# FFN input products of a two-layer trunk as seven block products, with a separate output stage

## The chip, the cores and the metric

One program runs on one core of one Trainium2 chip. The time is device microseconds (us) of one execution; less is better. TensorE (PE in the profile, its weight loads PEld) multiplies, VectorE (DVE), ScalarE (ACT) and GpSimd (POOL) do the elementwise work, SyncE (SP) issues most DMAs. All operands are float32 in DRAM.

## What is computed

The reference is a trunk of two layers over 1024 tokens of width 1024. Each layer has a token mixer (a gated DeltaNet, then a dilated window attention), and after it a SwiGLU feed-forward network (FFN) with 2816 hidden units. What the change touches is the FFN:

```python
h = (rms_norm(x, norm_ffn[layer]) * (1.0 + sc2) + sh2).astype(x.dtype)
x = x + g2 * swiglu(h, w_ffn_in[layer], w_ffn_out[layer])

def swiglu(h, w_in, w_out):
    gate, up = jnp.split(h @ w_in, 2, axis=-1)
    return (jax.nn.silu(gate) * up) @ w_out
```

## The kernel before

Activations are kept transposed: features on the 128 partitions, 512 tokens (one of two halves) along a row, so x is 2 x 8 tiles of 128x512. Every product is made in split float32: an operand is a pair of an upper part `hi` (ACT copies it, rounded to float32r) and a lower part `lo` (the rest, one subtraction in `lo_of`, which goes to DVE and to POOL in turn, since `lo_pool` is 2 in the FFN). `split3` sums upper x upper, upper x lower and lower x upper: three matmuls for each 128 of the contraction.

The FFN (`ffn`) goes through 22 tiles of 128 hidden units in groups of 2 or 3 (`FG`). For each tile `gate_up` multiplies gate and up weights with the first token half and then with the second, 24 matmuls of 128x128 by 128x512 into each PSUM bank, applies SiLU and the product with up, and splits the result for the next product. Once a group is through, its output products follow at once: 16 banks of three matmuls per tile, each added to x by one DVE instruction (L1141). In layer 0, `mods1` also works through the 96 pieces of the next layer's conditioning (one 256 KB load and one DVE instruction each, L221 and L223), three after each `gate_up`.

Which instruction stands where on each engine is decided by a scheduler at build time, from the order in the code; each engine then runs its own list strictly in order and waits on semaphores. While `PE.pinned` is set, PE's instructions keep the order of the code. Tiles come from pools with a fixed number of buffers, so a load can wait for the last reader of a buffer. `hlp` holds 32 tiles of 128x512, that is 16 pairs.

Of the kernel before, what the change touches and what calls it, by code (L numbers as in the profile page):

```python
# [17 lines left out]
P = 128  # L18
# [53 lines left out]
def trunk(tc, A, out, stop=None):  # L72
# [3 lines left out]
    class PE:  # L76
# [217 lines left out]
    def row_bcast(p, r, n=4):  # L294
# [3 lines left out]
        rb = p.tile([P, HALF], F32, name="rb", tag="rb", bufs=2)  # L298
        ACT.activation(rb, b, AF.Copy)
        return rb  # L300
# [155 lines left out]
    class OutProj:  # L456
# [51 lines left out]
        def late(self, tp, xp):  # L508
            w0 = [wunit(rows_cols(self.w_out, n * P, P), KT) for n in (3, 3 + 1)]
            self.ws = dict(zip((3, 3 + 1), w0))  # L510
            xT = [[xp.tile([P, HALF], F32, name="xt", tag="xt", bufs=16) for _ in range(KT)] for _ in range(2)]
# [3 lines left out]
            rb0 = row_bcast(tp, self.r0)  # L515
            stat = Stat(tp)
# [7 lines left out]
            return xT, [rb0, stat.r()]  # L524
# [573 lines left out]
    FG = [2, 2] + [3] * 6  # L1098

    def ffn(tp, xT, l, hT, tail, between=None):  # L1100

        w_i, w_o = A["w_ffn_in"][l], A["w_ffn_out"][l]
        t0 = 0
        for gi, gn in enumerate(FG):
            acts = [[None] * gn for _ in range(2)]
            wg = [None] * gn
            wo = []

            def gate_up(i, hf):
                t = t0 + i  # L1110
                if wg[i] is None:
                    wg[i] = (wunit(rows_cols(w_i, t * P, P), KT),
                             wunit(rows_cols(w_i, HID + t * P, P), KT))
                og, ou = pd(), pd()
                for o, w in ((og, wg[i][0]), (ou, wg[i][1])):
                    split3(o, [((w[0][:, k], w[1][:, k]), hT[hf][k]) for k in range(KT)])
                s = tp.tile([P, HALF], F32, name="sg", tag="ft")
                ACT.activation(s, og, AF.Silu)  # L1118
                V.tensor_tensor(s, s, ou, ALU.mult)  # L1119
                hi = tp.tile([P, HALF], F32R, name="ahi", tag="act", bufs=14)  # L1120
                lo = tp.tile([P, HALF], F32R, name="alo", tag="act", bufs=14)
                ACT.activation(hi, s, AF.Copy)  # L1122
                lo_of(lo, s, hi)
                acts[hf][i] = (hi, lo)
            order = [(i, hf) for i in range(gn) for hf in range(2)]
            if gi == 0:
                order = [(0, 0), (1, 0), (0, 1), (1, 1)]
            for i, hf in order:
                gate_up(i, hf)
                if between is not None:  # L1130
                    between()
            for i in range(gn):
                t = t0 + i
# [10 lines left out]
            t0 += gn  # L1144
    def toks(g, t):
# [22 lines left out]
    lo_pool, accs, araw = 2, 3, 3  # L1168
    with ExitStack() as fa:
        banks(pd="ab", pt="de", p0="a", p1="b", p2="c")  # L1170
        fw = fa.enter_context(pool("fw", 3))
        wpools(fw, 3, 1, 3)
        xp = fa.enter_context(pool("xp"))
        tp = fa.enter_context(pool("ft", 5))
        xT, rb = op.late(tp, xp)
        hT = [make_h(tp, 0, 1, xT[hf], rb[hf]) for hf in range(2)]
# [7 lines left out]

        ends = []
# [341 lines left out]
```

## Time and profile before

| | |
|---|---|
| three runs | 3048.33, 3054.59, 3058.15 us (median 3054.59) |
| the profiled execution | 3051.78 us, of which 3050.0 us lie between its first and last instruction (the span) |
| mean granted TensorE clock in it | 0.967 of full |

The rows further down come from this one execution. A row of busy times gives an engine's share of a stretch; a row of a timeline gives the start of a run of like instructions, how long it took, and in brackets how long the engine had been idle before it and whose work ended that.

### The profile page before, as it was taken

To read this page: it belongs to the slowest core of one execution; us is meant where nothing else is said; L and a number is where in the kernel's file an instruction comes from. 1 tells how busy PE (TensorE), PEld (TensorE's weight loads), DVE (VectorE), ACT (ScalarE), POOL (GpSimd) and SP (SyncE) were. 2 spreads that over 40 slices of the span, in tenths; PEclk is the share of its full clock that TensorE was granted. 3 is DMA by queue.
4 is the path that set the end of the run, shared out by engine and by line. 5 is a ranking of instruction groups with operands and counts; after the bars stand their busy time and mean duration, and the time that the engine had idled before them with its cause. 6 is when DMAs were issued, how large, how long until landed. Compare 5 with 4: busy or idle time off the path is not lost.

```text
span 3050.0 us, 39919 instructions
## 1 busy us (share of the span) xinstructions
PE 2900.4 (95%) x15831; PEld 2459.7 (81%) x15831; DVE 1375.7 (45%) x2799; ACT 877.3 (29%) x1779; POOL 667.1 (22%) x626
## 2 busy tenths in 40 slices
PE   6889888898989999999999999999979999999999
PEld 5777777776878888888879899999968888888887
DVE  7775676656686423222245342333276322332222
ACT  5432333333421211111134453443334121111111
POOL 2141323331211111111124122222212111111110
PEclk7989999999999999999999999999979999999999
DMA  7333332236765311111122301111222111111111
GB/s 252 96 94 115 105 87 66 55 100 187 234 205 156 104 42 49 40 58 49 49 80 81 99 29 41 52 50 44 77 91 73 45 56 42 50 41 55 49 35 59
DMA packets 271447, 250.91 MB, mean 82 GB/s; under 512 B 32035, under 2 KB 214563, under 8 KB 271260
## 3 DMA queue, kind: packets, MB, share of 16 engines
q1 hardware_dynamic: 265612, 234.77, 25.7%
q0 software_dynamic: 5648, 13.60, 1.5%
q8 instruction: 124, 2.03, 0.3%
q14 instruction: 63, 0.52, 0.1%
HBM read 218.70 MB, written 34.30 MB: 83 GB/s over the span
## 4 chain that ended last, share of the span: by engine, by line
PE 67%; DMA 3%; DVE 3%; issue 1%; ACT 0%; SPq 0%; POOL 0%; DVEq 0%; ACTq 0%; POOLq 0%
PE pd L82 59%; PE pt L82 3%; PE ob L82 2%; PE pp L82 1%; PE p L82 1%; DMA araw<-in_w_ada 1%; PE tq L82 1%; DMA b_d<-v_d 1%; DVE acc L223 1%; DVE w L157 0%; DMA gl<-og_d 0%; DVE ht L307 0%; DMA xt<-xs_d 0%; DVE hl L315 0%; DMA wraw<-in_dsw_w_in 0%
## 5 line engine op out<-in xcount | busy, mean ns | idle before, releaser
L82 PE MATMUL pd<-hl,w 128*128 128x512 f32 x6360 | 1550.1, 400 | 18.2 <-ACT w L183 9.1
L82 PEld LDWEIGHTS pd<-hl,w 128*128 128x128 f32 x6360 | 1196.4, 192 | 265.6 <-ACT w L183 9.7
L183 ACT ACTIVATE w<-wraw 128x512 fp32r<-128x512 f32 (+1 forms) x363 | 260.5, 730 | 877.2 <-PE pd L82 341.2
L157 POOL TENSOR_TENSOR w<-wraw,w 128x512 fp32r<-128x512 f32 (+1 forms) x135 | 225.9, 1675 | 1190.0 <-ACT w L183 1149.5
L82 PE MATMUL pd<-ahi,w 128*128 128x512 f32 x1408 | 451.5, 398 | 2.6 <-DVE xt L1141 2.6
L157 DVE TENSOR_TENSOR w<-wraw,w 128x512 fp32r<-128x512 f32 (+1 forms) x228 | 208.9, 919 | 386.9 <-ACT w L183 371.7
L82 PE MATMUL pd<-w,hl 128*128 128x256 f32 x2880 | 377.0, 286 | 0.0
L82 PEld LDWEIGHTS pd<-w,hl 128*128 128x128 f32 x2880 | 355.4, 192 | 7.2 <-issue 6.0
L82 PEld LDWEIGHTS pd<-ahi,w 128*128 128x128 f32 x1408 | 265.1, 188 | 66.2 <-DVE xt L1141 3.1
L82 PE MATMUL pd<-alo,w 128*128 128x512 f32 x704 | 279.4, 397 | 0.0
L1119 DVE TENSOR_TENSOR sg<-sg,pd 128x512 f32<-128x512 f32 x88 | 60.3, 685 | 383.6 <-PE pd L82 379.1
L82 PEld LDWEIGHTS pd<-alo,w 128*128 128x128 f32 x704 | 132.7, 188 | 31.3
L1141 DVE SCALAR_TENSOR_TENSOR qkv<-pd,modT,qkv 128x512 f32<-128x512 f32 x128 | 95.5, 750 | 128.6 <-PE pd L82 128.5
L223 DVE SCALAR_TENSOR_TENSOR acc<-araw,vecT,acc 128x512 f32<-128x512 f32 x140 | 113.3, 809 | 59.0 <-DMA araw<-in_w_ada 57.5
L1141 DVE SCALAR_TENSOR_TENSOR xt<-pd,modT,xt 128x512 f32<-128x512 f32 x128 | 95.0, 748 | 97.6 <-PE pd L82 97.4
L1118 ACT ACTIVATE sg<-pd 128x512 f32<-128x512 f32 x88 | 52.4, 596 | 242.4 <-PE pd L82 242.4
L1122 ACT ACTIVATE ahi<-sg 128x512 fp32r<-128x512 f32 x88 | 55.2, 627 | 221.8 <-DVE sg L1119 220.5
L682 DVE SCALAR_TENSOR_TENSOR yv<-raw,vecT,yv 128x512 f32<-128x512 f32 x144 | 112.6, 782 | 10.7 <-ACT yv L680 9.7
L135 POOL TENSOR_TENSOR ssa<-ssa,pw 128x8 f32<-128x8 f32 x48 | 80.7, 1682 | 165.8 <-DVE ssa L1304 154.5
L157 POOL TENSOR_TENSOR alo<-sg,ahi 128x512 fp32r<-128x512 f32 x46 | 67.0, 1456 | 212.3 <-ACT ahi L1122 212.2
L1346 DVE CUSTOM_DVE_ANT_0 p<-pt,bias 128x256 f32<-128x256 f32 (+1 forms) x192 | 61.6, 370 | 99.3 <-PE pt L82 63.4
L1352 ACT ACTIVATE p<-p,nm 128x256 f32<-128x256 f32 (+1 forms) x192 | 87.4, 457 | 36.8 <-DVE nm L1349 29.5
(285 smaller groups left out, 2746.5 us busy)
## 6 DMA issues: line engine op xcount, KB each, us to landing
araw<-in_w_ada SPq DMA_DIRECT2D x160, 256.0 KB, 2.9
wraw<-in_w_ffn_in SPq DMA_DIRECT2D x54, 512.0 KB, 3.9
wraw<-in_dsw_w_in SPq DMA_DIRECT2D x72, 256.0 KB, 2.9
wraw<-in_w_ffn_in SPq DMA_DIRECT2D x68, 256.0 KB, 2.9
wraw<-in_gdn_w_in SPq DMA_DIRECT2D x66, 256.0 KB, 2.9
wraw<-in_w_ffn_out SPq DMA_DIRECT2D x26, 512.0 KB, 3.8
wraw<-in_w_ffn_out SPq DMA_DIRECT2D x36, 256.0 KB, 2.6
araw<-in_w_ada SPq DMA_DIRECT2D x16, 512.0 KB, 8.4
```

What stands on the lines that cost most here:

```text
L82: i = f(*a, **k)
L135: G.tensor_tensor(o, i, pw[:, half, :n], ALU.pow)
L157: e.tensor_tensor(o, x, hi.bitcast(F32), ALU.subtract)
L183: ACT.activation(hi, raw, AF.Copy)
L223: V.scalar_tensor_tensor(acc, raw, condT[:, k:k + 1], acc, op0=ALU.mult, op1=ALU.add)
L682: V.scalar_tensor_tensor(yv, raw[:, i:i + HALF], convT[:, i, ct:ct + 1], yv, op0=ALU.mult, op1=ALU.add)
L1118: ACT.activation(s, og, AF.Silu)
L1119: V.tensor_tensor(s, s, ou, ALU.mult)
L1122: ACT.activation(hi, s, AF.Copy)
L1141: V.scalar_tensor_tensor(xt, o, modT[:, l, 5, n:n + 1], xt, op0=ALU.mult, op1=ALU.add)
L1346: V.tensor_tensor_reduce(p_[i][:, hp, c0:], lg[i][:, hp * 256 + c0:hp * 256 + 256], bias[:, h, c0:], 1.0, -3.0e38, ALU.add, ALU.max, orow[ ...
L1352: ACT.activation(p_[i][:, hp, c0:], p_[i][:, hp, c0:], AF.Exp, bias=nm[:, h:h + 1], accum_out=orow[:, h, DH + 1:DH + 2])
```

## The change

The gate and up weights of one hidden tile are taken as two rows of blocks (gate, up) by two columns (features 0 to 511, 512 to 1023), h as two rows of blocks (the same feature halves) by two columns (the token halves). The 2x2 block product is formed from seven block products (Winograd's form of Strassen's method) in place of eight, each of four 128-deep steps of three matmuls: 12 matmuls. Numbers 1 and 2 use blocks of weights and of the first token half as they are; 3, 4, 5, 6 and 7 need sums and differences of blocks of the weights, of h, or of both.

- `half0` makes h of the first token half (one DVE product with the row factors, one ACT instruction for the rest, in place in x) and its 8 pairs. `begin` then does products 1 and 2 of tiles 0 and 1.
- After that come the statistics of the second token half, its h, the block differences of h, and the 20 pairs of products 7, 6, 5, 3 and 4 (`half1`).
- `rest` does all other products in a written order, PE pinned. `weights` forms the weights' sums and splits them, `taken` empties the banks: partial results are copied out between products that go on adding to the same bank.
- The activations go to DRAM (`a_d`). Since x was overwritten by h, x goes to DRAM as well (`xs_d`) and comes back. All 22 tiles are through before the output stage (`ffn_out`) starts: it loads the activations, splits them, and multiplies in groups of 3 or 4 tiles.
- In layer 0 the conditioning pieces go one to a product from the ninth product of `rest` on, with two load buffers in place of three.

```diff
...
+        def then(cls, o, wh, wl, hh, hl, first, last):
+            cls.matmul(o, wh, hh, start=first, stop=False, skip_group_check=True)
+            cls.matmul(o, wh, hl, start=False, stop=False, skip_group_check=True)
+            cls.matmul(o, wl, hh, start=False, stop=last, skip_group_check=True)
...
-        def late(self, tp, xp):
-            w0 = [wunit(rows_cols(self.w_out, n * P, P), KT) for n in (3, 3 + 1)]
-            self.ws = dict(zip((3, 3 + 1), w0))
-            xT = [[xp.tile([P, HALF], F32, name="xt", tag="xt", bufs=16) for _ in range(KT)] for _ in range(2)]
+        def late(self, tp, w_from):
+            wcyc[0] = cycle([w_from])
+            self.ws = dict((n, wunit(rows_cols(self.w_out, n * P, P), KT)) for n in (3, 4))
+            xT = [[tp.tile([P, HALF], F32, name="xt", tag="ft") for _ in range(KT)] for _ in range(2)]
             for hf, ns in ((1, range(3)), (0, range(KT)), (1, range(3, KT))):
                 for n in ns:
                     SP.dma_start(xT[hf][n], xs_d[hf, n])
-            rb0 = row_bcast(tp, self.r0)
-            stat = Stat(tp)
+            rb0 = row_bcast(tp, self.r0, bufs=1)
+            stat = Stat(None, *(tp.tile([P, HALF], F32, name="sq", tag="ft") for _ in range(2)))
             for n in range(KT):
                 xt = xT[1][n]
                 if n < 3:
...
                 else:
                     self.one(n, 1, xt)
                 stat.add(xt)
-            return xT, [rb0, stat.r()]
+                G.dma_start(xs_d[1, n], xt)
+            return xT, rb0, stat
+    class FfnIn:
+        def __init__(self, l, ft, hx, fw, raws):
+            self.l, self.ft, self.hx, self.fw, self.raws = l, ft, hx, fw, raws
+            self.B = {x: [] for x in range(1, 8)}
+            self.st = [dict() for _ in range(NHT)]
+        def pair(self, x, far):
+            if far:
+                t = self.hx.tile([P, 2, HALF], F32R, name="hx", tag="hx")
+                hi, lo = t[:, 0], t[:, 1]
+            else:
+                hi, lo = hl_tile()
+            ACT.activation(hi, x, AF.Copy)
+            lo_of(lo, x, hi)
+            return hi, lo
+        def h(self, k, x, rb):
+            V.tensor_tensor(x, x, rb, ALU.mult)
+            ACT.activation(x, x, AF.Identity, bias=modT[:, self.l, 3, k:k + 1], scale=AT_[:, self.l, 1, k:k + 1])
+        def half0(self, xs, rb):
+            self.x0 = xs
+            for k in range(KT):
+                self.h(k, xs[k], rb)
+                self.B[1 if k < 4 else 2].append(self.pair(xs[k], False))
+        def half1(self, xs, rb):
+            x0, x1, ft = self.x0, xs, self.ft
+            for k in range(4):
+                self.h(k, x1[k], rb)
+                self.h(k + 4, x1[k + 4], rb)
+                V.tensor_tensor(x0[k], x1[k], x0[k], ALU.subtract)
+                V.tensor_tensor(x1[k], x1[k + 4], x1[k], ALU.subtract)
+                self.B[7].append(self.pair(x1[k], True))
+                ft.give(x1[k])
+            for k in range(4):
+                t = ft.take()
+                V.tensor_tensor(t, x1[k + 4], x0[k], ALU.subtract)
+                self.B[6].append(self.pair(t, True))
+                G.tensor_tensor(x0[k + 4], x0[k + 4], t, ALU.subtract)
+                ft.give(t)
+            for x, far, ts in ((5, True, x0[:4]), (3, False, x1[4:]), (4, False, x0[4:])):
+                for t in ts:
+                    self.B[x].append(self.pair(t, far))
...
+        def op(self, x):
+            w = self.fw.tile([P, 2, HALF], F32R, name="wo", tag="wo")
+            ACT.activation(w[:, 0], x, AF.Copy)
+            lo_of(w[:, 1], x, w[:, 0])
+            return w[:, 0], w[:, 1]
+        def weights(self, i, x):
+            s, ft = self.st[i], self.ft
+            if x in (1, 2):
+                if x == 1:
+                    s["rg"], s["ru"] = self.raw(i * P), self.raw(HID + i * P)
+                    w = s["w"] = wps.tile([P, 2, 1024], F32R, name="w", tag="w")
+                    ACT.activation(w[:, 0], s["rg"], AF.Copy)
+                    lo_of(w[:, 1], s["rg"], w[:, 0])
+                c = slice((x - 1) * HALF, x * HALF)
+                return s["w"][:, 0, c], s["w"][:, 1, c]
+            a11, a12, a21, a22 = (t[:, j * HALF:(j + 1) * HALF] for t in (s["rg"], s["ru"]) for j in range(2))
+            if x == 7:
+                t = ft.take()
+                V.tensor_tensor(t, a11, a21, ALU.subtract)
+                r = self.op(t)
+                ft.give(t)
+            elif x == 6:
+                s["s1"], s["s2"] = ft.take(), ft.take()
+                G.tensor_tensor(s["s1"], a21, a22, ALU.add)
+                V.tensor_tensor(s["s2"], s["s1"], a11, ALU.subtract)
+                r = self.op(s["s2"])
+            elif x == 5:
+                r = self.op(s["s1"])
+                ft.give(s["s1"])
+            elif x == 3:
+                V.tensor_tensor(s["s2"], a12, s["s2"], ALU.subtract)
+                r = self.op(s["s2"])
+                ft.give(s["s2"])
+            else:
+                r = self.op(a22)
+        def product(self, i, x):
+            s = self.st[i]
+            wh, wl = self.weights(i, x)
+            key = {2: "y", 4: "v", 7: "v"}.get(x, "u")
+            first, last = x in (1, 2, 7), x in (2, 3, 4)
+            if first:
+                s[key] = bank[key]()
+            for k, (hh, hl) in enumerate(self.B[x]):
+                c = slice(k * P, (k + 1) * P)
+                PE.then(s[key], wh[:, c], wl[:, c], hh, hl, first and k == 0, last and k == 3)
+            self.taken(i, x, s[key])
...
+        def begin(self):
+            for i in range(2):
+                for x in (1, 2):
+                    self.product(i, x)
+        def rest(self, between=None):
+            seq = [(i, x) for x in (7, 6, 5) for i in range(2)] + [(0, 3), (0, 4), (2, 1), (1, 3), (1, 4)]
+            for i in range(2, NHT):
+                seq += [(i, 7), (i, 6), (i, 2), (i, 5)] + [(i + 1, 1)] * (i + 1 < NHT) + [(i, 3), (i, 4)]
+            for n, (i, x) in enumerate(seq):
+                self.product(i, x)
+                if between is not None and n >= 8:
+                    between()
+    FG = [3, 4, 4, 4, 4, 3]
+    def ffn_out(l, xT, act_raw, tail):
...
+            wo, acts = [], [[], []]
+            for t in range(t0, t0 + gn):
+                for hf in range(2):
+                    r = act_raw()
+                    SP.dma_start(r, a_d[t, hf])
+                    hi, lo = hl_tile()
+                    ACT.activation(hi, r, AF.Copy)
+                    lo_of(lo, r, hi)
+                    acts[hf].append((hi, lo))
...
+            tp = f1.enter_context(pool("ft", 18))
+            xT, rb0, stat1 = op.late(tp, (wps, 1, (fw, "wraw", 4)))
+            ff = FfnIn(0, Slotted(tp), hx, fw, lambda: fw.tile([P, 1024], F32, name="wraw", tag="wraw", bufs=4))
+            ff.half0(xT[0], rb0)
+            banks(u="aad", v="b", y="c", pt="e")
+            PE.pinned = True
+            ff.begin()
+            PE.pinned = False
+            rb = row_bcast(tp, stat1.factors(tp.tile([P, 2, 4], F32, name="rst", tag="rst", bufs=1)), bufs=1)
+            ff.half1(xT[1], rb)
+            ends, calls = [], [0]
+            mods = [f for j in (1, 0, 2, 4, 3, 5)
+                    for f in mod_pieces(tp, 1, j, lambda f: ends.append((calls[0] + 3, f)), "ft")]
+            def mods1():
+                calls[0] += 1
+                while ends and ends[0][0] <= calls[0]:
+                    ends.pop(0)[1]()
+                if mods:
+                    mods.pop(0)()
+            PE.pinned = True
+            ff.rest(mods1)
+            while mods or ends:
+                mods1()
+            PE.pinned = False
+        fw = fa.enter_context(pool("fw", 6))
+        wpools(fw, 6, 1, 3)
+        tp = fa.enter_context(pool("ft", 8))
+        xT = [[xp.tile([P, HALF], F32, name="xt", tag="xt", bufs=16) for _ in range(KT)] for _ in range(2)]
+        for hf in range(2):
+            for n in range(KT):
+                SP.dma_start(xT[hf][n], xs_d[hf, n])
...
+    ff, ring = end["ff"], end["ft"]
+    with ExitStack() as f1:
+        banks(u="aad", v="b", y="c", pt="e")
+        ff.hx = f1.enter_context(pool("hx", 12))
+        ff.fw = fw = f1.enter_context(pool("fw", 6))
+        own = [lambda: fw.tile([P, 1024], F32, name="wraw", tag="wraw", bufs=2)] * 2
+        rcyc = cycle(own + [lambda r=r: r for r in end["raws"]])
+        ff.raws = lambda: next(rcyc)()
+        PE.pinned = True
+        ff.begin()
+        PE.pinned = False
+        rb = row_bcast(end["slots"], end["stat"].factors(ssx[:, :, 0:4]))
+        ff.half1(xT[1], rb)
+        PE.pinned = True
+        ff.rest()
...
```

Three places in the built order follow. `u`, `v` and `y` are PSUM banks of the block products, `hx` pairs of block differences of h, `wo` the split of a weight sum, `ft` scratch tiles, `ar` activations read back.

On PE at the start of layer 0's FFN, first before (the 171 begin with the last five output products of the mixer, 120 matmuls), then after the change:

```order
L82 MATMUL pd<-hl,w 128x512 x171
L82 MATMUL pt<-sq,sqa 128x1 x4
L82 MATMUL pd<-hl,w 128x512 x34
L82 MATMUL pt<-sq,rst 128x128 x4
L82 MATMUL pd<-hl,w 128x512 x11
```

```order
L82 MATMUL pd<-hl,w 128x512 x120
L82 MATMUL u<-hl,w 128x512 x12
L82 MATMUL y<-hl,w 128x512 x12
L82 MATMUL u<-hl,w 128x512 x12
L82 MATMUL y<-hl,w 128x512 x12
L82 MATMUL pt<-sq 128x1 x4
L82 MATMUL pt<-sq,rst 128x128 x4
L82 MATMUL v<-hx,wo 128x512 x24
```

The sums of the second half's statistics (`128x1`) stood after one product of the FFN with the first half, with more behind them; now they stand after everything that the first half alone allows, and products with `hx` are next.

On DVE and on POOL at the same place, after the change: from the row factors of the second half on (DVE), and from behind the square root of its statistics (POOL). L1156 and L1170 to L1178 are `half1` and `h`, L164 is `lo_of`, L1209 and L1214 the weights' sums:

```order
L1156 TENSOR_TENSOR xt<-xt,rb 128x512 x8
L1170 TENSOR_TENSOR xt<-xt 128x512 x3
L1171 TENSOR_TENSOR xt<-xt 128x512 x2
L164 TENSOR_TENSOR hl<-xt,hl 128x512
L1171 TENSOR_TENSOR xt<-xt 128x512
L1170 TENSOR_TENSOR xt<-xt 128x512
L164 TENSOR_TENSOR hx<-xt,hx 128x512
L164 TENSOR_TENSOR hl<-xt,hl 128x512
L1171 TENSOR_TENSOR xt<-xt 128x512
L1176 TENSOR_TENSOR ft<-xt 128x512 x4
L164 TENSOR_TENSOR hx<-xt,hx 128x512
L1209 TENSOR_TENSOR ft<-wraw 128x512 x2
```

```order
L164 TENSOR_TENSOR hl<-xt,hl 128x512 x2
L164 TENSOR_TENSOR hx<-xt,hx 128x512 x2
L1178 TENSOR_TENSOR xt<-xt,ft 128x512 x2
L164 TENSOR_TENSOR hx<-ft,hx 128x512
L1178 TENSOR_TENSOR xt<-xt,ft 128x512 x2
L1214 TENSOR_TENSOR ft<-wraw 128x512
L164 TENSOR_TENSOR hx<-ft,hx 128x512
L164 TENSOR_TENSOR hl<-xt,hl 128x512
L164 TENSOR_TENSOR hx<-xt,hx 128x512 x2
L164 TENSOR_TENSOR wo<-ft,wo 128x512
```

POOL's last row is the lower part of the weights of product 7 of tile 0, which PE's first run of `v<-hx,wo` reads in its third matmul. On DVE, six more lower parts follow the rows shown, the sixth that of product 7 of tile 1: 32 instructions in all. In layer 1, whose rows are not shown, DVE has 32 as well, and POOL 16 in front of the same row where it has 14 here.

On SP at the end of layer 0's input stage, before (weights of both products alternate), and after:

```order
L181 DMA wraw<-in_w_ffn_in 128x4x128 x3
L181 DMA wraw<-in_w_ffn_in 128x8x128 x3
L181 DMA wraw<-in_w_ffn_in 128x4x128 x4
L179 DMA wraw<-in_w_ffn_out 128x1024 x2
L181 DMA wraw<-in_w_ffn_in 128x8x128
```

```order
L1255 DMA a_d<-ft 128x512
L186 DMA wraw<-in_w_ffn_out 128x1024 x3
L1261 DMA a_d<-ft 128x512
L186 DMA wraw<-in_w_ffn_out 128x1024
L1368 DMA xt<-xs_d 128x512 x16
L1289 DMA ar<-a_d 128x512 x8
```

The store of the last tile's activations, and sixteen loads of x, now stand ahead of the first activation that is read back. The fourth `128x1024` load reuses the first one's buffer.

## Rows read from the trace of the kernel before

**Rows 1.** The page, busy time, share of the span and number of instructions.

```profile
PE 2900.4 (95%) x15831; PEld 2459.7 (81%) x15831; DVE 1375.7 (45%) x2799; ACT 877.3 (29%) x1779; POOL 667.1 (22%) x626
```

**Rows 2.** Stretches: length, busy PE, PEld, DVE, ACT, POOL; granted clock, DMA share, GB/s.

```profile
843.00:900.00 57.00, 53.04 (x248) 43.47 (x246) 44.63 (x68) 16.02 (x23) 9.91 (x6) 0.97 0.63 192
900.00:1400.00 500.00, 497.22 (x2191) 408.07 (x2192) 187.29 (x240) 84.91 (x124) 79.74 (x47) 1.00 0.26 78
...
2420.00:3000.00 580.00, 580.00 (x2533) 475.62 (x2532) 157.06 (x188) 99.98 (x146) 90.14 (x54) 1.00 0.15 45
```

**Rows 3.** Timeline of PE in layer 1: FFN input, and output product of the mixer.

```profile
2377.30 43.70 PE L82 MATMUL pd<-hl,w 128*128 128x512 f32 x192
2420.83 0.40 PE L82 MATMUL pd<-ahi,w 128*128 128x512 f32 x1
...
2270.20 5.74 PE L82 MATMUL pd<-hl,w 128*128 128x512 f32 x24
2275.78 0.38 PE L82 MATMUL pp<-sq,m 128*128 128x128 f32 x2
...
2292.79 29.27 PE L82 MATMUL pd<-hl,w 128*128 128x512 f32 x127
2321.90 0.94 PE L82 MATMUL pt<-sq,qkv 128*128 128x1 f32 x8
```

**Rows 4.** Timeline of layer 1's statistics of the second half, all engines.

```profile
2324.56 1.01 POOL L135 TENSOR_TENSOR rst<-rst,pw 128x4 f32<-128x4 f32 x1 [1.43 <-DVE rst L340]
...
2328.52 1.05 PE L82 MATMUL pt<-sq,rst 128*128 128x128 f32 x8
...
2329.61 0.60 ACT L299 ACTIVATE qkv<-pt 128x512 f32<-128x512 f32 x1 [0.47 <-PE pt L82]
```

**Rows 5.** The activations' lower parts: nanoseconds least/median/most, first and last start.

```profile
L157 POOL TENSOR_TENSOR alo<-sg,ahi x46: 1278/1295/2007, 864.1 to 3005.5; 128x512 fp32r<-128x512 f32 x46
L157 DVE TENSOR_TENSOR alo<-sg,ahi x42: 679/693/2574, 902.7 to 2994.6; 128x512 fp32r<-128x512 f32 x42
```

**Rows 6.** Timeline of DVE and POOL in layer 0.

```profile
826.54 0.75 DVE L307 SCALAR_TENSOR_TENSOR ht<-xt,modA,rb 128x512 f32<-128x512 f32 x1
...
826.88 3.87 POOL L157 TENSOR_TENSOR w<-wraw,w 128x1024 fp32r<-128x1024 f32 x1 [7.85 <-ACT w L183]
827.81 0.69 DVE L157 TENSOR_TENSOR w<-wraw,w 128x512 fp32r<-128x512 f32 x1
...
828.41 2.90 DVE L315 SCALAR_TENSOR_TENSOR hl<-ht,modT,hl 128x512 fp32r<-128x512 f32 x1
```

**Rows 7.** Groups by line and shape: busy us, mean ns, idle before.

```profile
L157 POOL TENSOR_TENSOR w<-wraw,w 128x1024 fp32r<-128x1024 f32 x41 | 102.4, 2500 | 423.4 <-ACT w L183 423.4
L183 ACT ACTIVATE w<-wraw 128x1024 fp32r<-128x1024 f32 x87 | 90.4, 1054 | 257.7 <-PE pd L82 138.4 <-issue 114.1 <-DMA wraw<-in_gdn_w_out 3.9
L1122 ACT ACTIVATE ahi<-sg 128x512 fp32r<-128x512 f32 x88 | 55.2, 627 | 221.8 <-DVE sg L1119 220.5 <-issue 0.8
L223 DVE SCALAR_TENSOR_TENSOR acc<-araw,vecT,acc 128x512 f32<-128x512 f32 x140 | 113.3, 809 | 59.0 <-DMA araw<-in_w_ada 57.5
```

**Rows 8.** SP's timeline where x is loaded; then DMA issues: KB each, us to landing.

```profile
799.95 4.44 SPq L514 DMA_DIRECT2D xt<-xs_d  x9
...
806.36 7.02 SPq L514 DMA_DIRECT2D xt<-xs_d  x7
...
wraw<-in_w_ffn_out SPq DMA_DIRECT2D x26, 512.0 KB, 3.8
...
xt<-xs_d SPq DMA_DIRECT2D x16, 256.0 KB, 5.1
```

**Rows 9.** PE before layer 1's FFN: timeline, then stretches as in rows 2.

```profile
2259.03 4.09 PE L82 MATMUL pd<-hl,w 128*128 128x512 f32 x10 [3.15 <-DVE hl L1424]
...
2240.00:2259.00 19.00, 4.80 (x19) 3.02 (x18) 17.33 (x57) 4.01 (x12) 4.85 (x4) 0.50 0.34 101
2259.00:2263.00 4.00, 3.97 (x11) 3.12 (x12) 3.24 (x20) 0.45 (x2) 0.48 (x1) 0.58 0.26 105
```

More of the change, by code (lines that the diff above doesn't have):

```diff
@@ L1095, in trunk, with __init__, take, give @@
         return
-    FG = [2, 2] + [3] * 6
-    def ffn(tp, xT, l, hT, tail, between=None):
-        w_i, w_o = A["w_ffn_in"][l], A["w_ffn_out"][l]
+    a_d = scratch("a_d", (NHT, 2, P, HALF))
+    class Ring:
+        def __init__(self, tiles):
+            self.tiles = list(tiles)
+        def take(self):
+            return self.tiles.pop(0)
+        def give(self, *ts):
+            self.tiles += ts
+    class Slotted:
+        def __init__(self, p):
+            self.p = p
+        def take(self):
+            return self.p.tile([P, HALF], F32, name="ft", tag="ft")
+        def give(self, *ts):
+            pass
@@ L1103, in ffn @@
+    FG = [3, 4, 4, 4, 4, 3]
+    def ffn_out(l, xT, act_raw, tail):
+        w_o = A["w_ffn_out"][l]
         t0 = 0
         for gi, gn in enumerate(FG):
[L1105 to L1133, printed above, removed]
+            wo, acts = [], [[], []]
[7 more added lines that the diff above has]
+                    acts[hf].append((hi, lo))
@@ L1183, in tail0 @@
                 rb[hf] = stat[hf].r()
-        ends = []
-        mods = [f for j in (1, 0, 2, 4, 3, 5) for f in mod_pieces(tp, 1, j, ends.append)]
-        def mods1():
-            due, ends[:] = ends[:1] if len(ends) > 1 or not mods else [], ends[1:] if len(ends) > 1 or not mods else ends[:]
-            for _ in range(3):
-                if mods:
-                    mods.pop(0)()
-            for f in due:
-                f()
-        ffn(tp, xT, 0, hT, tail0, mods1)
-        while mods or ends:
-            mods1()
-        if stop == "x0b":
-            spill_x(xT)
-            fa.close()
-            es.close()
-            return
+        ffn_out(0, xT, lambda: tp.tile([P, HALF], F32, name="ar", tag="ft"), tail0)
         hT = [make_h(tp, 1, 0, xT[hf], rb[hf], hf == 1) for hf in range(2)]
@@ L1426, in trunk @@
         op = OutProj(1, A["dsw_w_out"][0], src, 4)
-        xT, hT2, end = [[], []], [], {}
+        xT, end = [[], []], {}
         def x_slots(hf, kind):
@@ L1452, in half_done @@
                     stat[h2].add(xT[h2][n])
-                if h2 == 1 and not hT2:
+                    G.dma_start(xs_d[h2, n], xT[h2][n])
+                if h2 == 1 and len(ns) == 3:
                     rb = row_bcast(sl, stat[0].factors(rfac))
-                    hT2.append(make_h(sl, 1, 1, xT[0], rb))
+                    end["ff"].half0(xT[0], rb)
             end["stat"] = stat[1]
@@ L1475, in trunk @@
         return
+    ff, ring = end["ff"], end["ft"]
+    with ExitStack() as f1:
+        banks(u="aad", v="b", y="c", pt="e")
[11 more added lines that the diff above has]
+        ff.rest()
+        PE.pinned = False
     with ExitStack() as fa:
         banks(pd="ab", pt="cdce")
-        wpools(fa.enter_context(pool("fw", 3)), 3, 1, 3)
+        fw = fa.enter_context(pool("fw", 6))
+        wpools(fw, 6, 1, 3)
         tp = fa.enter_context(pool("ft", 5))
-        rb = row_bcast(end["slots"], end["stat"].factors(tp.tile([P, 2, 4], F32, name="rst", tag="rst")))
-        hT2.append(make_h(end["slots"], 1, 1, xT[1], rb))
+        ring.give(*(r[:, i * HALF:(i + 1) * HALF] for r in end["raws"] for i in range(2)))
+        xT = [[ring.take() for _ in range(KT)] for _ in range(2)]
+        for hf in range(2):
+            for n in range(KT):
+                SP.dma_start(xT[hf][n], xs_d[hf, n])
+        acyc = cycle([ring.take() for _ in range(6)])
         def tail1(hf, n):
@@ L1498, in tail1 @@
                 SP.dma_start(out[0, r0:r0 + P, (n - 3) * P:(n + 1) * P], ot)
-        ffn(tp, xT, 1, hT2, tail1)
+        ffn_out(1, xT, lambda: next(acyc), tail1)
     es.close()
```

58 lines of the change are left out of this document (45 added, 13 removed).

## The prediction

> **What bounds the kernel now.** I read the page's busy times first [rows 1]: PE is busy 95% of the span, the next engine 45%. So PE's own work is the time, and what counts is the number of matmuls and the stretches in which PE waits. The stretches come next [rows 2]: from 900 to 1400 us, most of layer 0's FFN, PE is busy 497.22 of 500; from 2420 to 3000, layer 1's, 580 of 580 at full granted clock; only the head of layer 0's FFN (843 to 900) has 3.96 us without a matmul. The reader should see that DVE (187 and 157 us) and POOL (80 and 90 us) have much room there on average. The timeline of PE gives the price of a matmul [rows 3]: 192 in 2420.83 - 2377.30 = 43.53 us, 0.2267 each.
>
> **What the change removes.** Before, gate and up take 22 x 96 = 2112 matmuls a layer; after, 22 x 7 x 12 = 1848. The output products stay at 1056. Products of 12 change the operand more often than groups of 24, and partial sums share banks with copies between. Two nearer rows bound the pace [rows 3]: 24 of the mixer's output product in 2275.78 - 2270.20 = 5.58 (0.2325 each), and 127 in 2321.90 - 2292.79 = 29.11 (0.2292). I take the middle one. Saved per layer: 2112 x 0.2267 - 1848 x 0.2292 = 478.8 - 423.6 = 55.2; both **110.4** (119.7 at 0.2267, 98.3 at 0.2325). This is certain in count, since the built order has these rows; only the pace is open. Whatever the change loses must be set against it.
>
> **The start of each input stage** is where I expect most of the loss. Before, four groups of 24 with the first half (96 matmuls, 22 us) stand between that half's h and the first use of the second; the order shows the statistics spread among them. After, `begin` has 48 (11 us), and the statistics' matmuls stand behind all of them. Then comes a chain in which PE has nothing else to do. First the row factors [rows 3, 4]: 0.94 (eight 128x1 sums, of which four stand here, 0.5), POOL 1.01, PE 1.05, ACT 0.60, with DVE's small step and five hand-overs of some 0.3 (0.47 in the one row that shows it): 4.7 us. Then everything that PE's third matmul of product 7 needs. PE runs its list in order, and that matmul reads the lower part of a weight difference which is POOL's fifteenth large row in layer 0, while the corresponding row of the second tile is DVE's thirty-second. The second comes right after 12 more matmuls, so both must be through.
>
> What a row costs is in [rows 5]: a lower part takes DVE 0.693 and POOL 1.295 at the median. DVE: 32 x 0.693 = 22.2. POOL: 15 x 1.295 = 19.4 (17 in layer 1: 22.0; its subtractions and sums of the same size I price alike). The question is whether the two run side by side. The same rows have tails: DVE's reaches 2.574, POOL's 2.007. One place shows why [rows 6]: POOL's 128x1024 row takes 3.87 in place of its mean of 2500 ns [rows 7], DVE's two-input row of 0.69 runs inside it, and the next three-input row takes 2.90 where its like took 0.75: it ended 831.31, behind POOL's end at 830.75. So in part they exclude each other. Side by side, with the order's dependences, the end is set by POOL's last eleven rows, which follow DVE's twentieth: 13.9 + 14.2 = 28.1 (layer 1: 13 rows of DVE, 9.0, and 16 of POOL, 20.7: 29.7). Taking turns, it is 22.2 + 19.4 = 41.6 (layer 1: 44.2). Before, most rows kept their median, but there DVE and POOL had idle time to miss one another; here both are handed work without a gap, and the row nearest to that is [rows 6]. I take turns.
>
> The Trainium skill, "SBUF — State Buffer", section "Who interferes with whom", says that a DVE instruction with two inputs in SBUF contends with a GpSimd instruction that reads SBUF, and that whoever issues first has the shared ports for the whole instruction. The tails and the 2.90 agree with it; the 0.69 that ran inside POOL's 3.87 fits it only if POOL was the one to stop. By it nearly all of these rows take turns (41.6); without it the sum would be 28.1, so it speaks against the change.
>
> Without matmuls then, layer 0: 4.7 + 41.6, less 1.8 in which PE itself computes statistics: **44.5** (31 side by side; 48.6 if six more DVE rows get ahead). Layer 1: **47** (33 to 51). ACT's 28 or so splits and h rows at 0.627 [rows 7] are 18 us and lie beside. What was idle in these stretches goes away: 3.96 + 2.78 = **6.7** back.
>
> In layer 1 the first half's h takes one ACT instruction more per tile, eight at 0.6 in front of the mixer's last bank evictions: **2** (0 to 4).
>
> **The transitions.** In layer 0, SP's list decides. Behind the store of the last activation (which waits for the last product) stand a 512 KB weight load that reuses a buffer, sixteen x loads and only then the first activation read back. The weight load must wait for its buffer: landing 3.8 [rows 8], ACT 1.05, POOL 2.5 [rows 7], some 8 with hand-overs. Issuing sixteen x loads took 813.38 - 799.95 = 13.4 in the kernel before [rows 8], where they also queued for transfer. Then an activation lands (3.8 to 5.1, the two loads of the same rows), and is split on ACT and DVE or POOL (0.63 + 0.7 to 1.3). In sum 8 + 13.4 + 5 + 2 = 28 to 29, less the 2 us of work that the last product's own emptying hides: **27** (19 if x issues overlap the buffer's wait, 32 with the slower ends). In layer 1 the order has the x loads scattered earlier; what stays is that output weights wait for PE's last reads of their buffers: 3.8 + 1.05 + two splits on POOL, 5: **9** (5 to 13).
>
> **The clock.** After idle stretches PE restarts slowly: 19 us with PE busy 4.80 had a granted clock of 0.50, half of full, that is 1.2 GHz, the next 4 us 0.58, and the first ten matmuls took 4.09 [rows 9] where ten at 0.2267 take 2.3. So 1.7 per restart, three restarts: **5** (4 to 7).
>
> **The rest of each input stage.** A tile is 84 matmuls, 19.2 us. Layer 0's DVE has seven two-input rows, 4.9, and about seven conditioning pieces at 809 ns [rows 7], 5.7; POOL four rows at 1.295 and one of 2.5, 7.7. Taking turns in full this is 18.2: 95% of the tile for some 14 tiles; without the pieces 12.5. So it fits barely. The other tight chain is from one emptied bank to its next use: between product 4 and the next tile's there are 2.75 us of matmuls for copies of 0.6 to 0.7 each. Stalls in all: **10** (0 to 40), a guess between no stall and 2 to 3 us in each of the 14 tight tiles.
>
> **Sum.** Lost: 44.5 + 47 + 27 + 9 + 5 + 10 + 2 - 6.7 = 137.8. Saved 110.4. Against the profiled execution's 3051.78 that is +27.4, 3079; the median of the runs is 2.8 above that execution, so I say **3080**. All bounds on one side: 31 + 33 + 19 + 5 + 4 + 0 + 0 - 6.7 - 119.7 = -34 (3020); on the other 48.6 + 51 + 32 + 13 + 7 + 40 + 4 - 6.7 - 98.3 = +91 (3145).
>
> **Rivals.**
> *A, faster: the two engines run side by side.* For it: most rows of before are at their median [rows 5]. Against it: [rows 6], and that nothing separates the rows here. Then the starts cost 31 + 33, 27.5 less, and the steady stage nothing: 137.8 - 27.5 - 10 = 100 lost, 10 below what is saved: 3044. The point of decision is a loss of 110.4: if the rows run side by side in both starts, that alone brings it there, and each cheaper term (the transition at 19, the pace at 0.2267) takes it down further, to 3027 with these two. Chance 0.22.
> *B, slower still: layer 0's stage is paced by DVE and POOL.* The 18.2 of 19.2 leaves out waits between rows and the late landing of conditioning loads, now with two buffers where the row for the pieces already waits 57.5 us on loads [rows 7]. With 2 us more in 14 tiles, +28 less the 10 in the sum's guess, and some more at the restarts: about 3104. Chance 0.15.
> *C, no change: the read back is hidden.* If the weight buffer is free early and the x loads issue at once, only the landing of an activation is left of the first transition, 5 in place of 27: 3058. The order speaks against it. Chance 0.08.
> *D, something not in this list,* such as a matmul pace at 0.2325 or above: 0.05.
>
> The forecast itself has 0.50, with a range of its own of 3060 to 3100. A measurement here tells apart about 0.3%, 9 us: so slower takes the forecast, B, and part of C and D (0.66), within takes part of A and C (0.14), faster the rest of A (0.20). The range for 8 in 10 goes from 3036, below A's centre, to 3118, beyond B's.
>
> **What the profile will show.** Right: in each layer, after 48 matmuls on `u` and `y`, PE idle for some 45 us, ended by POOL's or DVE's `wo` or `hx`, with DVE and POOL together busy nearly all of it and DVE's two-input means well above 693 ns; PE idle for some 27 us between the last `v` product and the first output product of layer 0, ended by an `ar` load and its split; 3696 matmuls into `u`, `y` and `v` at about 0.229; the granted clock at half after each. Wrong: DVE and POOL sums larger than the stretch they share (then they run side by side, and A's terms hold); a first transition under 10 us; gaps of 1 us or more at every tile, which would be B. The prediction falls if the two starts together cost under 65 us, or if a stall that I priced by the tile recurs in all 44.

## The result and the profile after

Median 3078.86 us (3076.87 to 3081.2, four runs) against 3051.62 of the kernel before on the same chip: ratio 1.0087, 95% interval 1.0066 to 1.0108, so 27 us slower, and 3080 was forecast. The profiled execution has a span of 3076.7, 26.7 more than before. The sum came out right, but not every term did. The page's first part, which answers to [rows 1]:

```profile
PE 2793.5 (91%) x15303; PEld 2372.6 (77%) x15303; DVE 1624.3 (53%) x3040; ACT 1058.5 (34%) x2097; POOL 995.9 (32%) x839
```

PE has 528 instructions fewer and less busy time, POOL half as much work again. Now the same stages, first the two FFNs before (columns as in [rows 2]), then after: each layer's input stage up to the first output product, and its output stage. Layer 0's FFN starts before 51 matmuls ahead of the end at 855.5, at 843.8; layer 1's 72 matmuls into the run of 127 of [rows 3], at 2309.3.

```profile
843.80:1594.12 750.32, 743.58 (x3297) 610.56 (x3296) 289.87 (x382) 142.32 (x210) 125.20 (x85) 1.00 0.27 82
2309.30:3050.00 740.70, 735.33 (x3250) 603.51 (x3248) 223.22 (x275) 135.43 (x199) 110.34 (x67) 1.00 0.16 50
```

```profile
850.77:1378.58 527.81, 446.77 (x1962) 364.58 (x1960) 306.88 (x369) 173.82 (x281) 207.81 (x129) 0.93 0.40 126
1378.58:1622.91 244.33, 244.17 (x1073) 201.89 (x1073) 124.75 (x145) 58.57 (x86) 74.29 (x51) 0.99 0.32 106
2339.75:2817.28 477.53, 426.24 (x1864) 350.26 (x1865) 214.72 (x256) 173.33 (x279) 207.46 (x129) 0.95 0.27 84
2817.28:3076.70 259.42, 251.09 (x1120) 206.82 (x1120) 118.71 (x137) 48.52 (x72) 59.02 (x32) 0.98 0.29 94
```

The FFNs take 1491.0 before and 1509.1 after: +18.1, of which layer 0 has +21.8 and layer 1 -3.8. PE's idle time goes from 12.1 to 140.8 (+128.7), its busy time from 1478.9 to 1368.3 (-110.6). The other 8.6 lie ahead: layer 0's FFN starts 7.0 later, and layer 1's mixer takes 1.6 more. Of the 7.0, 4.6 stand in the last 120 matmuls of layer 0's mixer, which take 34.2 in place of 29.6: ACT has more work beside them (17.7 us for 14.9), PE waits 2.20 and 0.73 for ACT's copy of a weight (`w` L190), and the granted clock is 0.90 there, 1.00 before.

Where PE stands at the start of layer 0's input stage (its timeline; in brackets the idle time before a run and what ended it):

```profile
861.65 0.95 PE L82 MATMUL pt<-sq 128*128 128x1 f32 x8
863.98 1.16 PE L82 MATMUL pt<-sq,rst 128*128 128x128 f32 x8 [1.38 <-POOL rst L142]
890.23 1.22 PE L82 MATMUL v<-hx,wo 128*128 128x512 f32 x2 [25.10 <-ACT wo L1192]
900.71 7.81 PE L82 MATMUL v<-hx,wo 128*128 128x512 f32 x22 [9.26 <-POOL wo L164]
908.36 2.88 PE L82 MATMUL u<-hx,wo 128*128 128x512 f32 x12
915.78 10.27 PE L82 MATMUL u<-hx,wo 128*128 128x512 f32 x36 [4.55 <-ACT wo L1192]
```

Together 40.3. The third matmul waits for POOL's `wo` row, as the order said. Layer 1 has 1.37, 30.57, 7.59 and 1.87 at the same places: 41.4. What the two engines do meanwhile, DVE first (its first eight rows, then the last ones ahead of POOL's `wo`), then POOL:

```profile
865.80 5.98 DVE L1156 TENSOR_TENSOR xt<-xt,rb 128x512 f32<-128x512 f32 x8 [1.84 <-ACT rb L306]
...
891.11 3.42 DVE L164 TENSOR_TENSOR hx<-ft,hx 128x512 fp32r<-128x512 f32 x2
894.46 3.41 DVE L164 TENSOR_TENSOR hx<-xt,hx 128x512 fp32r<-128x512 f32 x2
897.79 1.74 DVE L164 TENSOR_TENSOR hl<-xt,hl 128x512 fp32r<-128x512 f32 x1
```

```profile
892.28 1.71 POOL L164 TENSOR_TENSOR hx<-ft,hx 128x512 fp32r<-128x512 f32 x1
893.95 1.70 POOL L164 TENSOR_TENSOR hl<-xt,hl 128x512 fp32r<-128x512 f32 x1
895.62 3.37 POOL L164 TENSOR_TENSOR hx<-xt,hx 128x512 fp32r<-128x512 f32 x2
898.95 1.70 POOL L164 TENSOR_TENSOR wo<-ft,wo 128x512 fp32r<-128x512 f32 x1
```

Where both have rows, each engine starts one every 1.67 us, though the medians of before were 0.693 and 1.295 [rows 5]: neither is idle by its record, and neither is at its speed. Busy times and granted clock of this stretch (columns as in [rows 2]):

```profile
862.00:890.00 28.00, 1.76 (x14) 1.48 (x13) 25.05 (x28) 18.21 (x30) 14.67 (x10) 0.56 0.00 0
890.00:905.00 15.00, 5.51 (x12) 3.96 (x13) 13.55 (x10) 2.48 (x5) 13.61 (x9) 0.50 0.00 0
```

The transition in layer 0, on SP, ACT and PE:

```profile
1361.55 0.33 SPq L186 DMA_DIRECT2D wraw<-in_w_ffn_out  x1
1361.93 10.22 SPq L1368 DMA_DIRECT2D xt<-xs_d  x16
...
1372.48 5.06 SPq L1289 DMA_DIRECT2D ar<-a_d  x8
1377.89 5.38 ACT L1291 ACTIVATE hl<-ar 128x512 fp32r<-128x512 f32 x8 [10.89 <-DMA ar<-a_d]
...
1378.58 10.98 PE L82 MATMUL pd<-hl,w 128*128 128x512 f32 x36 [24.06 <-ACT hl L1291]
```

And one of seven gaps of 1.6 to 2.7 us in the rest of layer 0's input stage, 15.4 in all (16.7 with two of under 0.7), on DVE, ACT and PE:

```profile
1044.31 1.11 DVE L230 SCALAR_TENSOR_TENSOR acc<-araw,vecT,acc 128x512 f32<-128x512 f32 x1 [1.08 <-DMA araw<-in_w_ada]
...
1046.18 0.75 DVE L230 SCALAR_TENSOR_TENSOR acc<-araw,vecT,acc 128x512 f32<-128x512 f32 x1 [0.75 <-DMA araw<-in_w_ada]
1046.85 0.68 DVE L1209 TENSOR_TENSOR ft<-wraw 128x512 f32<-128x512 f32 x1
...
1047.62 1.76 ACT L1192 ACTIVATE wo<-ft 128x512 fp32r<-128x512 f32 x3 [4.12 <-DVE ft L1209]
...
1048.31 2.03 PE L82 MATMUL v<-hx,wo 128*128 128x512 f32 x5 [2.72 <-ACT wo L1192]
```

DVE waits for a conditioning load, and behind that piece stands the weight difference (L1209) that the next product 7 needs.

### The profile page after: what moved, and what is told of

It is laid out like the page before. It is cut to its first block, busy times and chain, and to the rows that moved or that the text cites. A ratio compares the mean times of both kernels' runs of the same rounds, so it can differ in the third digit from the quotient of the medians.

```text
span 3076.7 us, 40439 instructions
## 1 busy us (share of the span) xinstructions
PE 2793.5 (91%) x15303; PEld 2372.6 (77%) x15303; DVE 1624.3 (53%) x3040; ACT 1058.5 (34%) x2097; POOL 995.9 (32%) x839
## 4 chain that ended last, share of the span: by engine, by line
PE 62%; DMA 11%; DVE 10%; POOL 6%; issue 4%; ACT 3%; SPq 0%; DVEq 0%; POOLq 0%; ACTq 0%
PE pd L82 33%; PE u L82 11%; PE v L82 5%; PE pt L82 4%; DMA araw<-in_w_ada 4%; PE y L82 3%; PE ob L82 2%; POOL U L805 2%; POOL Ut L803 2%; DVE acc L230 2%; DMA wraw<-in_gdn_w_in 1%; PE pp L82 1%; PE p L82 1%; DMA E<-gs_d 1%; PE sc L82 1%
## 5 line engine op out<-in xcount | busy, mean ns | idle before, releaser
L82 PE MATMUL pd<-hl,w 128*128 128x512 f32 x4248 | 1082.9, 409 | 53.9 <-ACT hl L1291 24.8
L82 PEld LDWEIGHTS pd<-hl,w 128*128 128x128 f32 x4248 | 807.2, 196 | 223.0 <-ACT hl L1291 25.6
L164 POOL TENSOR_TENSOR w<-wraw,w 128x1024 fp32r<-128x1024 f32 (+1 forms) x102 | 201.3, 1975 | 358.2 <-ACT w L190 247.4
L190 ACT ACTIVATE w<-wraw 128x512 fp32r<-128x512 f32 (+1 forms) x229 | 159.1, 710 | 299.2 <-DMA wraw<-in_gdn_w_in 98.2
L82 PE MATMUL u<-hx,wo 128*128 128x512 f32 x1056 | 255.7, 392 | 6.4 <-ACT wo L1192 4.5
L82 PEld LDWEIGHTS u<-hx,wo 128*128 128x128 f32 x1056 | 199.0, 189 | 49.1 <-ACT wo L1192 5.0
L164 DVE TENSOR_TENSOR w<-wraw,w 128x512 fp32r<-128x512 f32 (+1 forms) x160 | 154.5, 969 | 132.7 <-ACT w L190 117.2
L82 PE MATMUL v<-hx,wo 128*128 128x512 f32 x528 | 137.5, 411 | 81.0 <-ACT wo L1192 63.5
L82 PE MATMUL u<-hl,wo 128*128 128x512 f32 x528 | 129.7, 395 | 12.0 <-ACT ft L1244 8.2
L82 PE MATMUL u<-hl,w 128*128 128x512 f32 x528 | 127.2, 390 | 1.8 <-DVE qkv L490 1.8
L82 PE MATMUL v<-hl,wo 128*128 128x512 f32 x528 | 127.5, 391 | 0.7 <-DVE qkv L1246 0.7
L82 PE MATMUL y<-hl,w 128*128 128x512 f32 x528 | 127.1, 390 | 0.0
```

What stands on the lines that cost most here:

```text
L82: i = f(*a, **k)
L164: e.tensor_tensor(o, x, hi.bitcast(F32), ALU.subtract)
L190: ACT.activation(hi, raw, AF.Copy)
```

## The experiments

Each kernel was timed against the kernel before on one chip; the ratio is to that one (the changed kernel: 1.0087). One thousandth is 3 us, and a difference of two ratios is uncertain by some 7 us, from both intervals together.

**Start on DVE alone.** In `half1`, and in the first six products of `rest`, no row goes to POOL:

```diff
-                G.tensor_tensor(x0[k + 4], x0[k + 4], t, ALU.subtract)
+                V.tensor_tensor(x0[k + 4], x0[k + 4], t, ALU.subtract)
...
+                lo_pool = 0 if n < 6 else 2
                 self.product(i, x)
```

> The changed kernel, but all rows that prepare the second half and the first six products of the rest (lower parts, differences, sums) are on DVE, none on POOL. Theory (the two engines take turns, so POOL's rows at about 1.1 us each block DVE): 47 DVE rows that follow each other at 0.60 are 28 us in place of the 34.9 from 865.8 to 900.7, so PE starts again some 6 us earlier in each layer, 12 in all: about 3067. Rival (they run side by side and DVE's list is the longer): 15 rows more on DVE are 9 us more per layer, about 3097. Second rival (ACT's splits set the end): within 3 us of 3079.

Ratio 0.9990 (0.9979 to 1.0002): some 30 us less, 24 less span. DVE and PE there:

```profile
867.26 4.90 DVE L1156 TENSOR_TENSOR xt<-xt,rb 128x512 f32<-128x512 f32 x8 [1.95 <-ACT rb L306]
...
893.76 0.67 DVE L164 TENSOR_TENSOR hl<-xt,hl 128x512 fp32r<-128x512 f32 x1
894.36 0.67 DVE L164 TENSOR_TENSOR wo<-ft,wo 128x512 fp32r<-128x512 f32 x1
```

```profile
888.64 1.22 PE L82 MATMUL v<-hx,wo 128*128 128x512 f32 x2 [22.05 <-ACT wo L1192]
895.09 7.78 PE L82 MATMUL v<-hx,wo 128*128 128x512 f32 x22 [5.23 <-DVE wo L164]
```

DVE goes from its first row at 867.26 to this `wo` without a gap, one row every 0.60: 27.8 us where the two engines took 34.8. Taking POOL away makes the whole faster, so the two do hinder each other, and by as much as taking turns would: the one POOL row that fell among DVE's first eight made them 1.08 longer (5.98 and 4.90), and 31 DVE rows at 0.60 with 15 POOL rows at 1.07 (1.67 - 0.60) are 34.7. PE's waits fall by 10.4 in layer 0 and 12.8 in layer 1, twice the 12 that I expected in all, since later rows come sooner too (PE's next wait in layer 0 falls from 4.55 to 1.3).

**Statistics early.** The sums stand behind the first product of `begin`, the broadcast behind the second:

```diff
+            self.product(0, 1)
+            r = stat()
+            self.product(0, 2)
+            rb = row(r)
```

> The changed kernel, but the sums of the second half's statistics stand behind the first of the four products of begin, and the broadcast of the row factors behind the second. Theory (what follows the row factors is one serial stretch, so it moves with them): the factors are there some 5 us earlier in each layer, PE's wait in front of product 7 shrinks by as much, 10 in all: about 3069. Rival (the rows then collide with the emptying of begin's banks, or PE waits for the sums): under 4 us in all.

Ratio 1.0034 (1.0022 to 1.0046): 16 less. The waits in layer 0 are 0.30, 21.50, 7.81 and 5.09 in place of 40.3 in all, in layer 1 0.35, 0.75, 26.11, 4.25 and 1.52 in place of 41.4 and a wait of 1.75 in front of `begin`: 5.6 and 10.2 less. Layer 0 gives what was expected; why layer 1 gives twice that was not settled.

**x behind the first activations.**

```diff
+            if gi == 0 and x_load is not None:
+                x_load()
```

> The changed kernel, but in layer 0 the sixteen loads of x are issued behind the first group's loads of activations in place of ahead of them. Theory (SP's list sets the transition): their 10.2 us of issuing leave the path, the gap of 24.1 us becomes 13 to 15, about 3069. Rival (the activations have to land after their store anyway, or the first output products then wait for x): the gap stays above 20, or what it loses comes back as waits of the first evictions for x; within 4 us of 3079.

Ratio 1.0061 (1.0037 to 1.0085), which overlaps the changed kernel's interval; the gap itself is plain, 13.18 in place of 24.06, and no wait for x comes in its place. The whole does not show it clearly: the profiled execution's span is only 1.2 shorter, since layer 1's mixer and input stage, whose code is unchanged, took 9 more in it. What is left of the gap is the output weights' load and split and one activation's landing.

**The three together.**

> The changed kernel with the three edits together: start on DVE alone, statistics early, x behind the first activations. If they add by what the traces showed of each alone (23 at the starts, 11 at the transition, 5.4 a layer for the statistics), the time is 45 below the changed kernel, about 3034, some 18 below the kernel before. Rival (statistics early overlaps with the start on DVE, since begin's banks are then emptied by a DVE that is full): 34 below, about 3045.

Ratio 0.9934 (0.9916 to 0.9953), 47 below the changed kernel: they add, within what the intervals can tell.

**The conditioning pieces.** First placed otherwise, alone and with the three edits:

```diff
-                if between is not None and n >= 8:
+                if between is not None and n >= 8 and x not in (3, 4):
```

> The changed kernel, but in layer 0 the conditioning pieces are not called behind products 3 and 4, so that DVE's weight difference for the next tile's product 7 has no piece that waits for its load ahead of it. Theory (the seven gaps of 1.6 to 2.7 us between 965 and 1222 come from that): 15 us of gaps become under 5, about 3069. Rival (the loads with two buffers are late anyway and the same waits stand elsewhere): within 3 us of 3079. If POOL and DVE's turns were the cause, no change either.

> The three edits and the placing of the conditioning pieces together. If the piece edit is worth 10 alone, it is worth 10 here: about 3024. If it is worth nothing, as the run with three.

Ratios 1.0111 (1.0093 to 1.013) and 0.9947 (0.9927 to 0.9968): no gain. That did not test the theory, since the edit did not do what I wanted: the scheduler again put runs of four pieces ahead of L1209, and PE's waits in the rest of the stage went from 16.7 to 20.2, now also later in it. So the loads themselves were taken away:

```diff
+                if held is None or len(held) < 2:
...
+                else:
+                    raw = held[k % 2]
```

> The changed kernel without 94 of layer 0's 96 loads of conditioning weights: the pieces keep their DVE instruction, but read the first two loaded tiles, so layer 1's conditioning is not the reference's. Theory (DVE stands at a piece whose load is late, with the next tile's weight difference behind it): the seven gaps of 1.6 to 2.7 us, 15 in all, and what the restarts after them cost go, about 3060. Rival (DVE and POOL have too much work in these tiles): the gaps stay, within 4 us of 3079.

Ratio 1.0035 (1.0022 to 1.0047), 16 less. From 925 to 1338, PE's busy time in this kernel:

```profile
925.00:1338.00 413.00, 411.66 (x1853) 340.72 (x1852) 250.50 (x321) 139.10 (x229) 165.80 (x105) 1.00 0.26 79
```

DVE and POOL are as busy as they were (250.5 and 165.8; 254.4 and 166.5 from 925 to 1354 in the changed kernel), and the gaps are gone: late loads made them, not too much work. Dividing the pieces between both stages:

> The run with three edits, with layer 0's conditioning pieces divided: 48 behind products 6, 2 and 5 of the input stage, 48 behind the banks of the output stage, one to a bank. If the late loads are what stalls the input stage, half as many there stall it for at most half as long: 8 to 15 us below the run with three, about 3024. Rival (the output stage's evictions then wait behind pieces whose loads are late): what is gained in the one is lost in the other, within 4 us of the run with three.

Ratio 0.9934 (0.9916 to 0.9953), as with three edits: the rival. Some 17 of waits stay in the input stage, fewer but up to 3.7 long, and 4.3 appear in the output stage behind DVE's evictions. Four load buffers instead:

```diff
-    lo_pool, accs, araw = 2, None, 2
+    lo_pool, accs, araw = 2, None, 4
...
-            fw = f1.enter_context(pool("fw", 6))
+            fw = f1.enter_context(pool("fw", 5))
```

> The changed kernel with four buffers for the conditioning loads of layer 0 in place of two; the room comes from the split weight sums, five in place of six. Without the loads the seven gaps were gone and the time 16 lower. Theory (two buffers make the loads late): most of the gaps go, 10 to 16 below the changed kernel, about 3066. Rival (a sixth split weight sum was needed, or the loads queue behind stores on SP): gaps of the same sum, within 4 us of 3079.

Ratio 1.0030 (1.0019 to 1.0041), 17 less. DVE's longest waits in the changed kernel (925 to 1350: waiter, what ended it, sum, times, longest) have the loads first; with four buffers (920 to 1330) they are 5.6 us, and PE is without a matmul for 3.5 (16.7 in the changed kernel):

```profile
DVE acc L230 <- DMA araw<-in_w_ada: 43.8, 37, 2.9
DVE ft L1249 <- PE y L82: 40.5, 12, 5.0
```

```profile
DVE ft L1246 <- ACT ft L1244: 48.9, 18, 4.2
...
DVE acc L230 <- DMA araw<-in_w_ada: 5.6, 6, 1.5
```

```profile
920.00:1330.90 410.90, 407.44 (x1836) 336.36 (x1834) 248.46 (x318) 138.03 (x228) 170.12 (x104) 1.00 0.44 136
```

So the loads were late for want of buffers.

> The run with three edits and the four load buffers: what the buffers give alone, below the run with three, about 3022; that would be 1% below the kernel before.

Ratio 0.9847 (0.9829 to 0.9864): 3007.92 against 3057.63, 50 us below the kernel before, and 73 below the changed kernel where the parts gave 47 and 17; it is some 17 below what I expected, and these runs can't tell whether more than the intervals is in that. Its timeline at the start of layer 0's input stage, and layer 0's waits from 838 to 1322, show what is left:

```profile
872.10 1.22 PE L82 MATMUL v<-hx,wo 128*128 128x512 f32 x2 [17.09 <-ACT wo L1192]
878.47 6.86 PE L82 MATMUL v<-hx,wo 128*128 128x512 f32 x22 [5.15 <-DVE wo L164]
```

```profile
PE v L82 <- ACT wo L1192: 17.3, 2, 17.1
PE pd L82 <- ACT hl L1297: 12.8, 1, 12.8
PE v L82 <- DVE wo L164: 6.8, 3, 5.1
```

**The pace of the output products,** a term that my sum had at zero. Before, 96 of them with nothing between stand from 2354.81 to 2377.30 [rows 3], 0.2343 each; after, 487 from 2849.69 on take 110.55 with the last one's whole length of 0.39, 0.2267 a start. The first of the 96, then the 487:

```profile
2354.81 0.40 PE L82 MATMUL pd<-ahi,w 128*128 128x512 f32 x1
```

```profile
2849.69 110.55 PE L82 MATMUL pd<-hl,w 128*128 128x512 f32 x487
```

In the built program the activations lay in bytes 187,904 to 220,672 of a partition (both layers together), each at a multiple of 64; now they lie below byte 77,152, 32 off such multiples. Two runs on the kernel before:

```diff
         tp = fa.enter_context(pool("ft", 5))
+        tp.tile([P, 8], F32, name="pad", tag="pad", bufs=1)
```

> The kernel before with one edit: a tile of 32 bytes a partition is put in front of the FFN's scratch pool, so that the activations' upper and lower parts lie 32 bytes further in SBUF; nothing else moves. In its trace the matmuls that read them follow one another every 0.234 us, those that read h every 0.2267, and the output stage of the changed kernel runs at 0.2267. Theory (where the tile lies sets the pace): 2112 matmuls get 7.5 ns cheaper, 16 us in all, about 3036. Rival (short groups of 6 to 9 matmuls in a bank set it): the pace stays at 0.234 and the time within 2 us of 3051.6.

```diff
-                hi = tp.tile([P, HALF], F32R, name="ahi", tag="act", bufs=14)
+                hi = act_p[0].tile([P, HALF], F32R, name="ahi", tag="act", bufs=14)
...
+        act_p[0] = fa.enter_context(pool("actp", 1))
```

> The kernel before, with the activations' upper and lower parts in a pool of their own ahead of the weights, some 92 KB lower in SBUF, in place of the scratch pool near its end. The 32 bytes of the run before left the pace at 0.233. Theory (the region of SBUF that the moving operand lies in, or what else works there, sets the pace): 0.2267, 2112 matmuls 7.5 ns cheaper, 16 us below the kernel before. Rival (something else in the order of these products): 0.233 to 0.234, and the time within 3 us of before.

Ratios 0.9988 (0.9977 to 0.9998) and 0.9961 (0.9947 to 0.9974). In the first the pace is 0.2333: the 32 bytes are not it. In the second, the same 96 matmuls:

```profile
2356.02 0.39 PE L82 MATMUL pd<-ahi,w 128*128 128x512 f32 x1
...
2377.78 7.42 PE L82 MATMUL pd<-hl,w 128*128 128x512 f32 x32
```

21.76 us, 0.2267 each. The order of the products is the same, so where the tiles lie sets the pace, and the kernel before would have gained 12 us from that alone. The edit also moved weights and scratch up by some 28 KB, so the activations' own place is not shown to be the cause. Their region by itself is not: in layer 1 of the changed kernel a pair of `hx` at bytes 189,792 to 193,888, where activations of layer 0 lay before, is read at 0.2268; of 1040 starts with that layer's activations 4 were under 0.230. What sets the pace stays open.

## Why the prediction was right

| term | forecast | measured |
|---|---|---|
| input products, both layers | -110.4 | -119.7 (0.2267 each, the low bound) |
| output products | 0 | -16 (2112 x 7.6 ns) |
| start, layer 0 and 1 | 44.5, 47 | 40.3, 41.4 (35.7, 39.5 up to the row that I priced) |
| transition, layer 0 and 1 | 27, 9 | 24.1, 8.4 (four waits: 5.35, 0.72, 1.32, 0.96) |
| rest of the input stages | 10 | 16.7 in layer 0, 4.5 in layer 1 |
| clock | 5 | a part of 25 (below) |
| idle time of before given back | -6.7 | -6.7 |
| ahead of the two FFNs | 2 | 8.6 |

With all of the 25 the measured terms add up to 26.6, the spans' difference.

**The mechanism of the starts was right, and its size too high.** I took turns over side by side. The stretch itself took 34.8, halfway between the 41.6 and the 28.1 that I had for the two, so the number does not decide; the run on DVE alone does. The 41.6 was the sum of all rows at their medians, but a pair took 1.67 and not 0.693 + 1.295. Up to the row that I priced, PE waited 35.7 and not 44.5 in layer 0; another 4.55 came behind it, a wait of product 6 that I had not seen. The Trainium skill's rule ("SBUF — State Buffer", "Who interferes with whom"), an exclusive lock, agrees with the run on DVE alone. That one engine can stop altogether shows in layer 1, in a POOL row that took 5.79 while DVE's rows followed each other at 0.60:

```profile
2364.71 5.79 POOL L1178 TENSOR_TENSOR qkv<-qkv 128x512 f32<-128x512 f32 x1 [4.30 <-DVE qkv L1176]
```

```profile
2365.10 0.68 DVE L1176 TENSOR_TENSOR qkv<-qkv 128x512 f32<-128x512 f32 x1
2365.70 0.68 DVE L164 TENSOR_TENSOR hl<-qkv,hl 128x512 fp32r<-128x512 f32 x1
...
2368.71 0.68 DVE L1171 TENSOR_TENSOR qkv<-qkv 128x512 f32<-128x512 f32 x1
```

One sign that I named was a bad one: DVE's and POOL's busy times sum to 66.9 in the 43 us from 862 to 905, which I said would mean side by side. A row that is held up counts as busy, so sums cannot tell the two apart.

**The transitions** went by their steps; issuing the x loads took 10.2 and not 13.4.

**The steady stage** was a guess without a mechanism, 10 for 21. I had priced DVE's and POOL's work; late loads stood beside it in rival B, without a price. What stalled layer 0 was the loads with two buffers, and a scheduler that put the pieces together. Layer 1 has no pieces, and its 4.5 were not looked into.

**Wrong terms cancelled.** The output products' pace, which I left out because their count does not change, gave 16, and the input products' pace 9 more than taken. Against these 25, PE's busy time fell by 110.6 only, where the two paces give 135.7: 25 us more, not 5, went into matmuls beside the gaps. From 890 to 905 twelve of them took 5.51, 0.46 each, at a granted clock of 0.50, which is 1.2 GHz; the clock was at that level in nine stretches of the two FFNs, at the long waits and at four of the short ones, where I had counted three restarts. The trace divides the 25: some 17 are the 87 large matmuls that began in those stretches (38.1 us; 19.7 at 0.2267 each) in place of 8 before, and some 3 the ends of runs before a gap, which no next matmul covers (0.39 - 0.2267 each). The other 5 were not settled. Of the other terms, the starts and transitions came out 13 cheaper than forecast, the steady stage and the time ahead of the FFNs 18 dearer. So the forecast came closer than its working deserved: had I seen only the gain it would have been 3055, only the loss 3100. (My own sum with the 2.8 on top is 3082; I wrote 3080.)

The loss was not in the seven products: without their stalls (three edits and four buffers) the same products beat the kernel before by 1.5%. Of that, the kernel before gains 0.4% from where its tiles lie, without any block product.

## What to carry to other kernels

A change that saves matmuls on an engine at 95% can lose all of it where the work that feeds the first of them has no cover: price the stretch between the last product that needs nothing new and the first that does, row by row, and try such two-input rows on DVE alone before spreading them over DVE and POOL back to back. Before blaming an engine's load for a stall, look at what its list waits for: here a second pair of load buffers was worth as much as moving the statistics. When a tile moves in SBUF, compare the start-to-start time of the matmuls that read it.

## What the hardware showed that I had not expected

Matmuls of 128x128 by 128x512 in one and the same order started every 0.2343 us with the moving operand (the 128x512) in bytes 187,904 to 220,672 of a partition, every 0.2333 with all of it 32 bytes further, and every 0.2267 with it in bytes 95,584 to 173,408 and other tiles moved up; the cause is open. Two lower parts on DVE and POOL that meet take 1.67 us for the pair, while DVE alone does two in 1.20: the second engine made the pair slower than the first alone.
